# Layer 0's first modulation weights in quarters with two projection blocks joined, and attention weights turned two rows behind their scores

## The chip, the cores and the metric

The kernel runs on one core of a Trainium2 chip. Its time is device microseconds of one execution. The engines are PE (matrix multiplies and transposes, results in PSUM), DVE (elementwise and reductions), ACT (activations and casts), POOL (gathers and small work), and SP, whose queue issues nearly all DMAs. A line number such as L246 is a line of the kernel before; lines of the changed kernel are named as such.

## The reference, cut to what matters

One step of a two-layer trunk over 128 context tokens and 512 latent tokens (640 rows, five token tiles of 128), model width 1024. Each layer is a mixer and an expert channel mixer (PEER), each behind a normalisation that is scaled and shifted by a modulation vector:

```python
sh1, sc1, g1, sh2, sc2, g2 = modulation(c, ada_w[l], ada_b[l])      # silu(c) @ w + b, 6 x 1024 columns
h = rmsnorm(xs, norm_mix_g[l]) * (1.0 + sc1) + sh1
# layer 0: aq, ak, av, bq, bk, bv, br, bg = split(h @ w_in)
#   A: windowed attention, 8 query heads on 2 key heads, softmax with a sink
#   B: gated linear attention in chunks of 64, scanned forwards and backwards
# layer 1: differential attention, 8 heads, two maps
xs = xs + g1 * o
xs = xs + g2 * peer(rmsnorm(xs, norm_ffn_g[l]) * (1.0 + sc2) + sh2, ...)
```

Context and latent rows have a modulation vector each, so a modulation is a product with two columns.

## The kernel before

Products of full precision are made of three passes: a matrix is split into a high part (ACT casts, `w_hi`, `hh`) and a low part (DVE subtracts, `w_lo`, `hl`), and `hi*hi`, `lo*hi`, `hi*lo` are added in PSUM. Normalised tokens are kept transposed, `hh` and `hl`, in eight chunks of 128 features.

`mix0` is layer 0's mixer. Its front works in this order. `Stats` squares the tokens chunk by chunk and adds (ACT and DVE), `end` sums over features on PE (`stin`, L178), and `rs_rows` spreads the reciprocal root over the partitions (`dg` on DVE, `rb` on PE, L203). `ada_half` (L110 to L131) makes the first third of layer 0's modulation in two halves: 8 tiles of 512 KB each, every one two DMAs (L118) into a pool of three buffers, two matmuls a tile (`adap`, L121), a copy of the row (L124), transposes (`adah`, L127), and the addition of the bias (`mods`, L131). `fold_gain` and `norm_mod` (L210 to L213) then give the four chunks of that half, on DVE and ACT. After the first half, four of the five token tiles of projection block 0 (256 query columns) take their first four chunks (`first`, L246); the rest follows when the second half is done.

The projection is in blocks of 256 columns. `proj_t` (tokens on partitions: blocks 0 and 1 queries, 2 keys and values, 3 and 4 values of B; `et`, L246) makes 24 matmuls a token tile; `rope.unit` normalises and rotates queries and keys on DVE, and PE turns them (`utp`, L448). `proj_f` (features on partitions, `ef`, L435) gives B's queries, keys and output gate. The order is blocks 0, 1, 2, the gate `bg` and `z`, then `proj_f(0)`, `proj_f(1)`, blocks 3 and 4, `proj_f(2)`, `proj_f(3)`. A weight block of 1 MB is loaded (L218), cast and split (`wload`, L219, L220).

The next stage has 20 units of attention A (a query block and a pair of heads) in rows r = 0 to 24, in PE's order as written. In a row: `a_scores` (`S`, L552), `a_soft` (maxima on DVE, exponentials on ACT L581, division on DVE L589), the transposes of the weights of unit r-1 (`a_turn`, `PT`, L598, copied by ACT to `pt`), the product of unit r-2 (`a_out`, `oA`, L611). Between them stand B's parts: `scan_setup` (cumulative gates `bT`, L632, and `kps`) in rows 3k and 3k+1, `scan` in row 3k+2 (products `kvb`, L683, then nine dependent DVE steps into `ss`, L688), `b_out` from row 12 (`aT` L704, `oB`, `ost` L738, `orb` L748). `fill` steps give PE the other modulation thirds: each step is a 512 KB tile (`adaw`, L91; `adap`, L94) out of three buffers; the last step loads and splits the first block of the output projection, whose first product is `ewops` (L335).

Layer 1's attention begins with `CS` (L1016), the maximum `cm` on DVE and the exponential `CP` on ACT. Ahead of its first cycle `proj.load(0)` loads output weights and splits them at once (`w_hi` L219 on ACT, `w_lo` L220 on DVE).

## Times and profile before

| | us |
|---|---|
| three runs | 4010.91, 4010.84, 4004.29 |
| median of the runs | 4010.84 |
| profiled execution, its own time | 4004.18 |
| its span | 4002.4 |
| PE busy | 3874.9 (97%) |
| DVE, ACT, POOL busy | 2951.8, 1553.3, 730.9 |
| chain that ended last | PE 75%, DVE 15%, ACT 4%, DMA 3% |

The runs lie on two levels 0.17% apart, and the profiled execution is on the lower one. A busy share says how long an engine had an instruction in it; what a stage costs is read from the idle time of the engine on which it ends, and from the event that ended that idle time. In timelines a row may stand for several records; a matmul of 32-bit operands leaves two records. The granted clock is the share of TensorE's full 2.4 GHz; 0.50 is 1.2 GHz.

### The profile page before, as it was taken

How to read it: one execution, taken by the hardware profiler on the slowest of the kernel's cores; microseconds unless marked ns; L12 is line 12 of the kernel's file. 1: busy time of each engine (PE TensorE's matmuls, PEld its weight loads, DVE VectorE, ACT ScalarE, POOL GpSimd, SP SyncE). 2: the span in 40 equal slices, each digit the busy share in tenths (PEclk: the TensorE clock that was granted, in tenths of full speed). 3: DMA queues.
4: the chain of work that ended last, by engine and by line, in shares of the span. 5: the costliest groups of instructions: out<-in, count | busy, mean ns of one | idle time of the engine just before them, and what ended most of it. 6: DMA issues, size and time to landing. Idle time of an engine off the chain costs nothing.

```text
span 4002.4 us, 55592 instructions
## 1 busy us (share of the span) xinstructions
PE 3874.9 (97%) x20858; PEld 3191.0 (80%) x20858; DVE 2951.8 (74%) x6091; ACT 1553.3 (39%) x2310; POOL 730.9 (18%) x687
## 2 busy tenths in 40 slices
PE   7989999999999999999999899999999999999998
PEld 5958887888788888888877678788878888888887
DVE  5255389996778778777775663999967777787775
ACT  3344235666332323323343553356562323223231
POOL 0000000000334333333200110000003333343432
PEclk9999999999999999999999999999999999999999
DMA  5144134557888888888553012455568888888884
GB/s 181 55 168 143 54 123 170 202 198 255 287 281 296 284 289 304 272 298 285 199 184 107 17 38 70 131 181 202 196 252 294 280 296 297 278 301 276 294 296 169
DMA packets 363922, 850.70 MB, mean 213 GB/s; under 512 B 27858, under 2 KB 172164, under 8 KB 356868
## 3 DMA queue, kind: packets, MB, share of 16 engines
q1 hardware_dynamic: 289012, 576.04, 41.3%
q0 software_dynamic: 74640, 271.10, 19.6%
q8 instruction: 164, 2.69, 0.3%
q14 instruction: 106, 0.87, 0.1%
HBM read 738.12 MB, written 108.92 MB: 212 GB/s over the span
## 4 chain that ended last, share of the span: by engine, by line
PE 75%; DVE 15%; ACT 4%; DMA 3%; issue 2%; POOL 1%; SPq 0%; DVEq 0%; ACTq 0%; POOLq 0%
PE O L1568 11%; PE O L1564 11%; PE O L1565 11%; PE S L1177 8%; PE S L1178 7%; PE S L1180 7%; PE ow L929 4%; PE pqs L1236 2%; PE et L246 2%; DVE ul L220 2%; DMA gr<-Sd 1%; PE ef L435 1%; PE ewops L335 1%; PE owops L335 1%; PE adap L94 1%
## 5 line engine op out<-in xcount | busy, mean ns | idle before, releaser
L1177 PE MATMUL S<-h2h,uh 128*128 128x512 f32 x2048 | 811.0, 396 | 13.2 <-ACT uh L219 5.7
L1564 PE MATMUL O<-Wh,vh 128*128 128x512 f32 x2048 | 798.5, 390 | 6.2 <-ACT Wh L1527 4.5
L1178 PE MATMUL S<-h2l,uh 128*128 128x512 f32 x2048 | 798.8, 390 | 0.0
L1565 PE MATMUL O<-Wh,vl 128*128 128x512 f32 x2048 | 797.9, 390 | 0.0
L1568 PE MATMUL O<-Wl,vh 128*128 128x512 f32 x2048 | 782.2, 390 | 0.0
L1180 PE MATMUL S<-h2h,ul 128*128 128x512 f32 x2048 | 589.2, 389 | 0.0
L219 ACT CAST vh<-v_raw 128x1024 fp32r<-128x1024 f32 x256 | 269.7, 1053 | 804.0 <-PE O L1568 779.8
L1471 POOL DMA_INDIRECT gv<-in_pv_dram,eidx x256 | 362.5, 1416 | 799.2 <-DVE acc L1487 773.7
L1177 PEld LDWEIGHTS S<-h2h,uh 128*128 128x128 f32 x2048 | 385.3, 188 | 98.9 <-ACT uh L219 12.3
L1564 PEld LDWEIGHTS O<-Wh,vh 128*128 128x128 f32 x2048 | 385.0, 188 | 88.1 <-ACT Wh L1527 6.5
L1568 PEld LDWEIGHTS O<-Wl,vh 128*128 128x128 f32 x2048 | 385.3, 188 | 80.4
L1565 PEld LDWEIGHTS O<-Wh,vl 128*128 128x128 f32 x2048 | 385.2, 188 | 79.5
L1180 PEld LDWEIGHTS S<-h2h,ul 128*128 128x128 f32 x2048 | 384.3, 188 | 79.8
L1178 PEld LDWEIGHTS S<-h2l,uh 128*128 128x128 f32 x2048 | 385.5, 188 | 76.6
L220 DVE TENSOR_TENSOR ul<-u_raw,uh 128x1024 fp32r<-128x1024 f32 x256 | 312.2, 1220 | 181.1 <-ACT uh L219 138.9
L1471 POOL DMA_INDIRECT gu<-in_pu_dram,eidx x256 | 320.6, 1252 | 514.6 <-DVE dots L1478 366.5
L219 ACT CAST uh<-u_raw 128x1024 fp32r<-128x1024 f32 x256 | 269.2, 1052 | 336.8 <-PE S L1178 299.6
L220 DVE TENSOR_TENSOR vl<-v_raw,vh 128x1024 fp32r<-128x1024 f32 x256 | 312.4, 1220 | 117.3 <-ACT vh L219 116.2
L1487 DVE SCALAR_TENSOR_TENSOR acc<-gv,dots,acc 128x1024 f32<-128x1024 f32 x256 | 327.7, 1280 | 44.5 <-DMA gv<-in_pv_dram,eidx 43.7
L1478 DVE CUSTOM_DVE_ANT_0 gu<-gu,h2p 128x1024 f32<-128x1024 f32 x256 | 311.2, 1219 | 43.9 <-DMA gu<-in_pu_dram,eidx 43.5
L1402 ACT ACTIVATE stg<-G 128x512 f32<-128x512 f32 x256 | 261.1, 1162 | 0.6 <-PE G L1400 0.6
L1465 POOL MEMSET acc<- 128x1024 f32 x2 | 1.9, 958 | 1335.2 <-DVE oj L1385 757.3
(404 smaller groups left out, 5617.4 us busy)
## 6 DMA issues: line engine op xcount, KB each, us to landing
u_raw<-in_uT_dram SPq DMA_DIRECT2D x256, 512.0 KB, 5.0
v_raw<-in_vR_dram SPq DMA_DIRECT2D x256, 512.0 KB, 6.7
gt<-Gd SPq DMA_DIRECT2D x64, 1024.0 KB, 7.4
Gd<-stg SPq DMA_DIRECT2D x30, 2048.0 KB, 8.5
adaw<-in_adaw_dram SPq DMA_DIRECT2D x80, 512.0 KB, 4.1
Sd<-ge SPq DMA_DIRECT2D x144, 256.0 KB, 3.3
gr<-Sd SPq DMA_DIRECT2D x134, 256.0 KB, 8.7
owr<-in_ow_dram SPq DMA_DIRECT2D x12, 1024.0 KB, 6.5
```

Source lines behind the costliest of these rows:

```text
L219: nc.scalar.copy(hi, raw)
L220: nc.vector.tensor_tensor(lo, raw, hi.bitcast(F32), op=OP.subtract)
L1177: nc.tensor.matmul(ps, hi[:, c], h2h[:, c], start=(c == 0), stop=False)
L1178: nc.tensor.matmul(ps, hi[:, c], h2l[:, c], start=False, stop=False)
L1180: nc.tensor.matmul(ps, lo[:, c - 5], h2h[:, c - 5], start=False, stop=(c == NC + 5 - 1))
L1402: nc.scalar.activation(stg[0][:, :, t0:t0 + 4].rearrange("p i t -> p t i"), ps, AF.Copy, scale=1.0 / GSC)
L1471: nc.gpsimd.indirect_dma_start(out=r[:], out_offset=None, in_=I[table], in_offset=bass.IndirectOffsetOnAxis(ap=eidx2[:, k:k + 1], axis=0))
L1478: nc.vector.tensor_tensor_reduce(r, r, h2p, 1.0, 0.0, OP.mult, OP.add, dots[:, k:k + 1])
L1487: nc.vector.scalar_tensor_tensor(acc, r, dots[:, k:k + 1], acc, op0=OP.mult, op1=OP.add)
L1564: nc.tensor.matmul(ps, hi[:, order[y]], Wh, start=(y == 0), stop=False)
L1565: nc.tensor.matmul(ps, lo[:, order[y]], Wh, start=False, stop=False)
L1568: nc.tensor.matmul(ps, hi[:, x], Ws[n // NC * CH + x][1], start=False, stop=(y == CH + lag - 1))
```

## The change

Three places change; the experts, layer 1's projections and all outputs are computed as before.

1. **The front.** The modulation third comes in four quarters of 8 tiles of 256 KB. All 32 tiles have a place of their own in tiles that are still unused then (`rooms`: the later homes of qA, br, bv, lg, qB, kB and the `adaw` buffers), but for the fourth quarter, which takes the places of the first again. Two chunks are normalised behind each quarter. Blocks 0 and 3 are loaded side by side as 512 columns (`eload`, four chunks at a time), and `emm` multiplies chunk by chunk for all five token tiles, in PE's order as written. The sums over features stand behind the first quarter's matmuls. Blocks 1, 4, 2 follow. There are five PSUM buffers of a bank in place of four.
2. **Attention A with B.** The scan stands at the start of its row, the weights of unit r-2 are turned (before: r-1), the product is that of unit r-3, and each row has 2 fill steps, 5 from row 22 on. Buffers: 5 `Pm`, 4 `pt`, 4 `adaw`, 1 `ktt`; several short-lived tiles share one place.
3. **Layer 1's attention.** The first output weights are loaded ahead (`fetch`) and split at the end of cycle 5.

```diff
-    def ada_half(h, ap, ps, out):
+    def ada_quarter(n, ps, out, tiles, arow):
-        for c in range(NC):
-            if c == 4:
-                yield
-            w = ap.tile([P, 2, 512], F32, name=f"adax{h}_{c}", tag="adaw", bufs=3)
-            for k in range(2):
-                nc.sync.dma_start(w[:, :, k * 256:k * 256 + 256], I["adaw"][0, 0, c, k, :, h::2])
+        for c, w in enumerate(tiles):
+            nc.sync.dma_start(w, I["adaw"][0, 0, c, n % 2, :, n // 2::2])
+        yield
+        r = slice(n % 2 * 64, n % 2 * 64 + 64)
+        for c, w in enumerate(tiles):
             for x in range(2):
-                p0 = h * 64 + x * 32
-                nc.tensor.matmul(ps[p0:p0 + 32], sc[:, c], w[:, x], start=(c == 0), stop=(c == NC - 1))
+                p0 = r.start + x * 32
+                nc.tensor.matmul(ps[p0:p0 + 32, :256], sc[:, c], w[:, x], start=(c == 0), stop=(c == NC - 1))
...
+                def eload(h):
+                    lo, hi = [wp.tile([P, 4, 512], F32R, name=f"e{x}{h}", tag=f"w{x}", bufs=2) for x in "lh"]
+                    raw = wp.tile([P, 4, 512], F32, name=f"er{h}", tag="wr", bufs=1)
+                    for k, b in enumerate((0, 3)):
+                        nc.sync.dma_start(raw[:, :, k * 256:k * 256 + 256], I["ewt"][b][:, h * 4:h * 4 + 4])
+                    store_split(hi, lo, raw)
+                    return hi, lo
...
+                def quarter_end(n):
+                    next(qs[n])
+                    fold_gain(0, 1, gmix, amix[0], n * 2, n * 2 + 2)
+                    norm_mod(0, amix[0], 0, hh, hl, tp, rb, n * 2, n * 2 + 2)
...
+                    def emm(c, tts):
+                        hi, lo = ew[c // 4]
+                        for tt in tts:
+                            a = (slice(None), c, slice(tt * P, (tt + 1) * P))
+                            for k, (x, y) in enumerate(((hh, hi), (hl, hi), (hh, lo))):
+                                nc.tensor.matmul(first[tt], x[a], y[:, c % 4], start=(c == 0 and k == 0),
+                                                 stop=(c == NC - 1 and k == 2))
+                    for n in range(3):
+                        emm(n * 2, range(NT))
+                        if n == 0:
+                            next(qs[3])
+                        next(qs[n + 1])
+                        emm(n * 2 + 1, (0, 1))
+                        quarter_end(n + 1)
+                        emm(n * 2 + 1, (2, 3, 4))
+                    for tt in range(NT):
+                        emm(6, (tt,))
+                        emm(7, (tt,))
...
-                for b in range(3):
+                for tt, ps in enumerate(first):
+                    tsl = slice(tt * P, (tt + 1) * P)
+                    nc.scalar.copy(bv[:, tt, :256], ps[:, 256:])
+                    qk(ps, 0, 0, tt, f"00_{tt}", qA[:, 0:2, tsl])
+                for b in (1, 4, 2):
                     proj_t(b)
...
                 proj_f(1)
-                proj_t(3)
-                proj_t(4)
...
                 for r in range(25):
-                    if r < len(us):
-                        a_scores(us[r])
+                    if r in sq:
+                        scan(*sq[r])
                     for g in row.get(r, []):
                         next(g)
                     if r < len(us):
+                        a_scores(us[r])
                         a_masks(us[r])
                         a_soft(us[r])
-                    if 0 <= r - 1 < len(us):
-                        a_turn(us[r - 1], 0)
+                    if 0 <= r - 2 < len(us):
+                        a_turn(us[r - 2], 0)
                     for g in full.get(r, []):
                         next(g, None)
-                    for _ in range(3 if r % 3 == 0 else 2):
+                    if 0 <= r - 2 < len(us):
+                        a_turn(us[r - 2], 1)
+                    for _ in range(2 if r < 22 else 5):
                         next(fill, None)
-                    if 0 <= r - 1 < len(us):
-                        a_turn(us[r - 1], 1)
-                    if 0 <= r - 2 < len(us):
-                        a_out(us[r - 2])
-                    if r in sq:
-                        scan(*sq[r])
+                    if 0 <= r - 3 < len(us):
+                        a_out(us[r - 3])
...
-                proj.load(0)
+                fins.append(proj.fetch(0))
...
-                        if p_ in (len(units), len(units) + 1):
+                        if p_ in (5, len(units), len(units) + 1):
                             fins.pop(0)()
```

The DMAs of the front as they stand in SP's queue, first before, then now (`adax`, and now `qA` to `adax`, are the modulation tiles; `w_raw` and `er` are projection weights):

```order
L118 DMA adax_0_163<-in_adaw_dram 128x2x256 x2
L118 DMA adax_1_168<-in_adaw_dram 128x2x256 x2
L118 DMA adax_2_173<-in_adaw_dram 128x2x256 x2
L218 DMA w_raw<-in_ewt_dram 128x2048
L118 DMA adax_3_178<-in_adaw_dram 128x2x256 x2
L118 DMA adax_4_212<-in_adaw_dram 128x2x256 x2
```

```order
L114 DMA qA_108<-in_adaw_dram 128x2x256 x4
L114 DMA br_109<-in_adaw_dram 128x2x256 x4
L420 DMA er_183<-in_ewt_dram 128x4x256 x2
L114 DMA bv_110<-in_adaw_dram 128x2x256 x4
L114 DMA lg_111<-in_adaw_dram 128x2x256 x4
L420 DMA er_198<-in_ewt_dram 128x4x256 x2
L114 DMA qB_112<-in_adaw_dram 128x2x256 x2
L114 DMA kB_113<-in_adaw_dram 128x2x256 x2
```

Two quarters, 16 pieces, are now ahead of the second projection load (`er_198`), and the third and fourth quarters stand behind it; that load goes into the one `er` buffer and so waits until the first is split.

PE in rows 2 and 3 of the attention stage, before and now (`S` scores, `PT` turned weights, `bT` gates of the next scan, `kvb` products of the scan, `oA` output, `adap` a fill tile):

```order
L598 MATMUL PT_1_0_1977<-ident,P_1_0_1918 128x128
L94 MATMUL adap_1_1890<-adaw_1_2_1_1981,sc 32x256 x4
L94 MATMUL adap_1_1890<-adaw_1_3_0_1987,sc 32x256 x4
L598 MATMUL PT_1_1_1993<-ident,P_1_1_1920 128x128
L611 MATMUL oA_1997<-pt_0_0_1930,av 64x128
L611 MATMUL oA_1997<-pt_0_1_1956,av 64x128
L683 MATMUL kvb_2001<-bv,ktt_1932 64x128 x16
L683 MATMUL kvx_2002<-bv,ktt_1932 64x128 x2
L552 MATMUL S_3_0_2031<-kA,qA 128x128
L552 MATMUL S_3_1_2032<-kA,qA 128x128
L598 MATMUL PT_2_0_2050<-ident,P_2_0_1967 128x128
L632 MATMUL bT_2054<-tri,lg 128x128 x5
```

```order
L740 MATMUL kvb_1859<-bv,ktt_1836 64x128 x16
L740 MATMUL kvx_1860<-bv,ktt_1836 64x128 x2
L609 MATMUL S_2_0_1889<-kA,qA 128x128
L609 MATMUL S_2_1_1890<-kA,qA 128x128
L655 MATMUL PT_0_0_1908<-ident,P_0_0_1776 128x128
L655 MATMUL PT_0_1_1912<-ident,P_0_1_1778 128x128
L94 MATMUL adap_1_1804<-adaw_1_2_0_1916,sc 32x256 x4
L94 MATMUL adap_1_1804<-adaw_1_2_1_1922,sc 32x256 x4
L609 MATMUL S_3_0_1928<-kA,qA 128x128
L609 MATMUL S_3_1_1929<-kA,qA 128x128
L655 MATMUL PT_1_0_1947<-ident,P_1_0_1826 128x128
L689 MATMUL bT_1951<-tri,lg 128x128 x5
```

Between `kvb` and the next `bT` stood the scores of one row and one transpose; now the scores of two rows, three transposes and two fill tiles stand there, and `PT` takes weights whose scores lie two rows back.

PE at the end of the stage, before and now (`ost` and `orb` belong to the last tile of B's output):

```order
L611 MATMUL oA_3290<-pt_3_0_3400,av 64x128
L611 MATMUL oA_3290<-pt_3_1_3430,av 64x128
L738 MATMUL ost_3499<-ones,obt 128x1 x4
L102 MATMUL adap_0_3014<-ident,adar_0_3511 128x8 x4
L748 MATMUL orb_3518<-obt,ones 128x128 x4
L335 MATMUL ewops_3548<-oh_1815,ewo_h 128x320
```

```order
L668 MATMUL oA_3232<-pt_3_0_3313,av 64x128
L668 MATMUL oA_3232<-pt_3_1_3337,av 64x128
L805 MATMUL orb_3407<-obt,ones 128x128 x4
L94 MATMUL adap_0_3127<-adaw_0_6_1_3415,sc 32x256 x4
L94 MATMUL adap_0_3127<-adaw_0_7_0_3421,sc 32x256 x4
L94 MATMUL adap_0_3127<-adaw_0_7_1_3427,sc 32x256 x4
L102 MATMUL adap_0_3127<-ident,adar_0_3433 128x8 x4
L344 MATMUL ewops_3462<-oh_1729,ewo_h 128x320
```

Three fill tiles and the modulation's transposes (L102) now stand between the last `orb` and `ewops`; before, all fill tiles were ahead of this `oA`.

## Rows read from the trace of the kernel before

**Rows 1.** The page, part 2: PE busy, 40 slices of 100 us.

```profile
PE   7989999999999999999999899999999999999998
```

**Rows 2.** Waits of PE, 0 to 118 us: total us, times, longest.

```profile
PE adap L121 <- DMA adax<-in_adaw_dram: 7.1, 7, 2.7
```

**Rows 3.** Waits of the SP queue from 0 to 130 us.

```profile
SPq L118 <- PE adap L121: 16.1, 12, 6.4
```

**Rows 4.** Groups of PE, 205 to 372 us: busy, mean ns, idle before.

```profile
L94 PE MATMUL adap<-adaw,sc 128*32 128x256 f32 x384 | 26.6, 396 | 2.9 <-DMA adaw<-in_adaw_dram 2.4 <-DVE mods L104 0.6
L598 PE MATMUL PT<-ident,P 128*128 128x128 f32 x120 | 22.3, 298 | 4.7 <-DVE P L589 4.6
...
L552 PE MATMUL S<-kA,qA 64*128 64x256 f32 (+2 forms) x80 | 18.1, 464 | 4.0 <-ACT P L581 3.3 <-ACT br L479 0.7
...
L748 PE MATMUL orb<-obt,ones 128*128 128x128 f32 x40 | 7.2, 339 | 4.0 <-DVE obt L744 4.0
L632 PE MATMUL bT<-tri,lg 128*128 128x128 f32 x40 | 6.6, 321 | 8.7 <-DVE ss L688 3.4 <-DVE mx L577 2.9 <-DVE mx L584 2.5
...
L704 PE MATMUL aT<-qd,kd 64*128 64x128 f32 x80 | 5.5, 277 | 2.7 <-DVE ss L688 2.7
```

**Rows 5.** Windows: us; busy PE, PEld, DVE, ACT, POOL; PE clock, DMA, GB/s.

```profile
8.00:20.00 12.00, 6.18 (x26) 5.20 (x28) 4.56 (x10) 5.24 (x7) 0.00 (x0) 1.00 0.91 310
38.00:42.00 4.00, 4.00 (x15) 1.76 (x11) 4.00 (x10) 2.45 (x6) 0.00 (x0) 0.60 0.79 245
55.00:60.00 5.00, 3.22 (x12) 1.78 (x8) 1.77 (x7) 0.58 (x1) 0.00 (x0) 0.50 0.64 228
...
2226.00:2240.00 14.00, 11.75 (x40) 7.45 (x41) 10.72 (x25) 6.10 (x15) 4.06 (x15) 0.52 0.11 39
```

**Rows 6.** DMA issues: count, KB each, median us to landing.

```profile
adaw<-in_adaw_dram SPq DMA_DIRECT2D x80, 512.0 KB, 4.1
...
adax<-in_adaw_dram SPq DMA_DIRECT2D x32, 256.0 KB, 3.9
```

**Rows 7.** Timeline, 8 to 56 us: start, us, operation, [idle before, released by].

```profile
9.29 4.41 SPq L118 DMA_DIRECT2D adax<-in_adaw_dram  x6
...
12.92 2.29 PE L178 MATMUL stin<-ones,sqin_acc 128*128 128x1 f32 x10 [12.92 <-DVE sqin_acc L172]
...
17.91 1.07 DVE L201 TENSOR_SCALAR dg<-ident,rsn 128x128 f32<-128x128 f32 x5
...
33.05 1.05 PE L121 MATMUL adap<-adax,sc 128*32 128x512 f32 x4 [0.72 <-DMA adax<-in_adaw_dram]
...
36.55 1.01 DVE L210 SCALAR_TENSOR_TENSOR nxr<-xT,amix,rb 128x128 f32<-128x128 f32 x2
...
40.24 1.00 DVE L210 SCALAR_TENSOR_TENSOR nxr<-xT,amix,rb 128x128 f32<-128x128 f32 x2
...
53.57 2.29 DVE L220 TENSOR_TENSOR w_lo<-w_raw,w_hi 128x2048 fp32r<-128x2048 f32 x1 [9.56 <-ACT w_hi L219]
```

**Rows 8.** Timeline of PE: last tile of block 0, and 512-column matmuls elsewhere.

```profile
70.05 0.39 PE L246 MATMUL et<-w_hi,hh 128*128 128x256 f32 x1 [1.21 <-DVE ua L283]
...
2216.25 0.39 PE L929 MATMUL ow<-owh,hh 128*128 128x512 f32 x1
2216.48 0.39 PE L929 MATMUL ow<-owh,hl 128*128 128x512 f32 x1
```

**Rows 9.** The chain of waits, 60 to 210 us: start, us, what.

```profile
148.76 28.80 PE et L246 x240
```

**Rows 10.** Timeline of PE, end of that stage.

```profile
370.02 0.61 PE L335 MATMUL ewops<-oh,ewo_h 128*128 128x320 f32 x1
```

**Rows 11.** Timeline, 2224 to 2227 us, start of layer 1's attention.

```profile
2224.56 1.04 ACT L219 CAST w_hi<-w_raw 128x1024 fp32r<-128x1024 f32 x1 [2.52 <-DMA w_raw<-in_owo_dram]
...
2225.64 1.23 DVE L220 TENSOR_TENSOR w_lo<-w_raw,w_hi 128x1024 fp32r<-128x1024 f32 x1 [0.98 <-ACT w_hi L219]
...
2226.44 2.50 PE L1016 MATMUL CS<-kC,qC 64*128 64x320 f32 x8 [3.22 <-ACT CP L1030]
```

More of the change, by code (lines that the diff above doesn't have):

```diff
@@ L96, in ada @@
                 yield
-        row = ap.tile([P, 512], F32, name=f"adar{l}_{q}", tag="adar", bufs=1)
+        row = (arow or (lambda nm: ap.tile([P, 512], F32, name=nm, tag="adar", bufs=1)))(f"adar{l}_{q}")
         nc.scalar.copy(row, ps)
@@ L391, in mix0 @@
                 tp = s2.enter_context(tc.tile_pool(reuse_waits="tile", name="t0", bufs=2))
-                with ExitStack() as s3:
-                    sp = s3.enter_context(tc.tile_pool(reuse_waits="tile", name="st0", bufs=2))
-                    st = Stats.pooled("in", sp, PP.tile([P, 512], F32, "stin", "b1"), None)
-                    for c in range(NC):
-                        st.add(c)
-                    aps = ada_ps(0, 0)
-                    halves_ = [ada_half(h, ap, aps, pp.tile([P, 2, P], F32, name=f"adah{h}", tag="tr", bufs=1)[:, 0])
-                               for h in range(2)]
-                    next(halves_[0])
-                    st.end()
@@ new lines, in mix0 @@
+                with tc.manual_schedule(engines={mybir.EngineType.PE}):
+                    with ExitStack() as s3:
+                        sp = s3.enter_context(tc.tile_pool(reuse_waits="tile", name="st0", bufs=2))
+                        st = Stats(PP.tile([P, 512], F32, "stin", "b1"),
+                                   act.tile([P, T], F32, name="sqin_acc", tag="bg"),
+                                   lambda c: sp.tile([P, T], F32, name=f"sqin_{c}", tag="sq", bufs=2), None)
+                        for c in range(NC):
+                            st.add(c)
+                        next(qs[0])
+                        ew = [eload(0)]
+                        next(qs[1])
+                        ew.append(eload(1))
+                        next(qs[2])
+                        next(qs[0])
+                        st.end()
+                    rs_rows("0", tp, rb)
+                    quarter_end(0)
+                    first = [PP.tile([P, 512], F32, f"et0_{tt}", "b1") for tt in range(NT)]
+                    def emm(c, tts):
[16 more added lines that the diff above has]
+                        emm(7, (tt,))
@@ L513, in ada_rest @@
                 for l, q in ((0, 1), (0, 2), (1, 0)):
-                    yield from ada(l, q, ap, ada_ps(l, q), 3)
-                hi, lo = [ap.tile([P, NC, P], F32R, name=f"ewo_{x}", tag="adaw", bufs=3) for x in "hl"]
-                w_first.extend(split(ap, hi, lo, I["ewo"][0], P, "ewo", 3, tag="adaw"))
+                    yield from ada(l, q, ap, ada_ps(l, q), 4, arow)
+                hi, lo = [ap.tile([P, NC, P], F32R, name=f"ewo_{x}", tag="adaw", bufs=4) for x in "hl"]
+                w_first.extend(split(ap, hi, lo, I["ewo"][0], P, "ewo", 4, tag="adaw"))
                 yield
```

88 lines of the change are left out of this document (47 added, 41 removed).

## The prediction, made before the changed kernel ran

> **What bounds the kernel now.** I read the page's slices first: PE is the engine on which nearly every slice ends, and only the first four of forty are below nine tenths for it, so a change in layer 0's mixer is worth what it takes out of PE's idle time there [rows 1]. Second the waits of PE in the front: 7.1 us in seven waits for modulation tiles [rows 2]. SP's own waits tell why they are late: it stood 16.1 us, twelve times, until a matmul had freed one of three tile buffers [rows 3]. Third the groups of PE in the attention stage, 205 to 372 us. Their idle times are 2.9, 4.7, 4.0, 4.0, 8.7 and 2.7, together 27.0 us: the next scan's gates `bT` and the first `aT` wait for DVE, which is still in the scan or the maxima, `PT` waits for the divided weights, the last `orb` for the last product of B [rows 4]. Fourth the granted clock: after stretches with waits TensorE runs at 1.2 GHz for a while, 0.60 on average from 38 to 42 us, 0.50 from 55 to 60 [rows 5]. So the bound is not PE's work but the order in which it gets its operands.
>
> **The front, step by step.** The eight pieces of the first quarter are issued 4.41/6 = 0.735 us apart from 9.29 on, the last at 14.4, and land 3.9 us later, at about 18.5 [rows 6, 7]. By the 310 GB/s that flowed from 8 to 20 us their 2.1 MB would take 6.8 us, so issue and landing decide, not the rate [rows 5].
>
> The Trainium skill's page "DMA: Bandwidth & Descriptors", section "Bandwidth", asks for batches of 1 MiB and gives 138 GB/s for a transfer of 64 KB; it would speak against 32 pieces of 256 KB. By an estimate from that figure the four quarters would take 61 us, the fourth would land at 70, and the joined blocks would end near 83 in place of 80 (below). The trace disagrees for pieces of this size: 310 GB/s with several in flight [rows 5].
>
> A tile of 512 columns costs PE 1.05 us, so one of 256 half of it, 0.53, and a quarter 4.2 [rows 7]. The first ends at 19. The sums over features, before begun at 12.92, now stand behind it. From their begin to the end of `dg` it took 18.98 - 12.92 = 6.1 us, so `dg` now ends at 25.1, and with the spreading, the bias and the gains DVE could normalise from 27 [rows 7]. There the low half of the first projection weights stands ahead of it, 2.29 us for a tile of 2048 elements a partition, the size of the new one [rows 7]. The first joined matmul starts at about 32. From there PE has 120 matmuls of 512 columns, 0.23 apart (2216.25 to 2216.48), 27.6 us [rows 8], and three quarters, 12.6: together 40.2, to 72 if nothing waits.
>
> It will wait. From the end of a half's last tile (33.05 + 1.05) to the first normalising instruction there are 2.45 us, and two chunks take 40.24 - 36.55 = 3.7 on DVE, half of that until the first is ready: 4.3 us, against 15 matmuls (3.4 us) that stand beside them [rows 7]. About 1 us a quarter stays open, 3 in all; the fourth leaves 1 more, since both of its chunks must be ready for the last matmuls. Block 1's weights are cast and split meanwhile on ACT and DVE, ahead of the fifth chunk: 4 more (2.29 on DVE and a like time on ACT). I get 32 + 40 + 8 = 80. One fall of the clock as at 55 us, five microseconds at half rate, is likely among these waits; it adds 2.5, so 82.5 [rows 5].
>
> The end to compare it with: before, the last token tile of block 0 began at 70.05 and took 24 matmuls and two transposes, to 73.1 [rows 8]. Blocks 3 and 4 took 28.80 us later, 14.4 for one, 0.12 a matmul [rows 9]. As block 3 is now inside the joined blocks, break-even is 73.1 + 14.4 = 87.5, and the front gains 5.0. Doubling the columns is worth only 120 x (2 x 0.12 - 0.23), about 1 us of it. Bounds: 79 (one wait fewer, no fall of the clock), and 99 if DVE's chain and a cold clock add up; so -8.5 to +11.5.
>
> SP has all 32 pieces behind each other, and the second projection load waits in the queue until the first is split; the third and fourth quarters stand behind it. If the split is at 29.4, 1 MB and 2.1 MB at 310 GB/s land by 40, and PE asks for the third quarter at about 48: hidden by 8 us. The evacuation of five joined tiles (DVE) lies beside block 1's matmuls, since `first` holds five buffers; if it didn't, one wait like the 1.21 at 70.05 would come [rows 8].
>
> **Attention A with B.** Work for PE is unchanged, so I balance its idle time. A whole row now lies between scan and `bT`, and between scores and `PT`: 8.7 + 2.7 + 4.7 go [rows 4]. What is late next: the scores of the next row wait for the exponentials of this one, since `S` has two buffers and fewer instructions stand between. Such waits were 3.3 us in three, 1.1 each [rows 4]; one in each of the four cycles until row 12 is 4.4. In rows 2, 5, 8 and 11 nothing stands between the two halves of `PT`, so the second waits for ACT's copy; no row has this wait, it lies between 0 and PT's mean wait, 4.7/4 = 1.2, and I take 0.8, 3.2 in all. The first `S` and the modulations stay, 1.3.
>
> The stage's end has a new load: 11 fill tiles in the last three rows. With four buffers, 4.1 us to land and 26.6/48 = 0.55 us on PE, a tile comes every 1.16 us: 12.8 us, of which PE works about 8 [rows 4, 6]. Then the first output weights are loaded into the same buffers, cast and split, of which some 4 us are open before `ewops`, which began at 370.02 [rows 10]. That makes 8.5 in place of the 4.0 of `orb` and 2.4 of the `adaw` waits. Sum 4.4 + 3.2 + 1.3 + 8.5 = 17.4, against 27.0: -9.6. Bounds: no new wait and the end as before, 5.3 of idle, -21.7; eight rows that wait the longest seen, 1.9 each, +1.
>
> **Layer 1's attention.** The cast of output weights waited 2.52 us for its DMA and took 1.04 on ACT, ahead of the first exponential; `CS` waited 3.22 for it [rows 11]. Between 1.04 and 3.22 go; I take 1.8. Its later place, in cycle 5, costs 0 to 1.2 (DVE's 1.23), I take 0.6 [rows 11]. From 2226 to 2240 the clock was 0.52 with 11.75 us of PE work [rows 5]; a shorter wait may save up to 5.6, I count 1. Together -2.2.
>
> **Sum.** -5.0 - 9.6 - 2.2 = -16.8. Against the profiled execution, 4004.2, that is 3987; the median, 4010.8, lies on the upper of two levels of the runs and would give 3994. I take the middle, 3991.
>
> **Rivals.** First, the front gains nothing: DVE's chain of splits and normalising is longer than I made it, and the joined blocks end at 87.5. For it, DVE has four splits of weights and eight chunks there; against it, 8 us of waits are already counted. Then -11.8, 3996. Second, attention's waits only change their owner: the longest waits are as good as any softmax with two `S` buffers can have, and the end of the stage costs more. For it, `S` already waited for `P`; against it, the largest waits were DVE's order, not ACT's pace. Then -7.2, 4000. Third, the clock: PE works in bursts of 3 to 4 us between waits, as it did with single tiles before 38 us, when the clock fell. If the clock stays at 1.2 GHz from 32 us on, the 40.2 us become 80.4, the joined blocks end at 112, and the front loses 25: +13, 4021. It decides from 99.3 on, when 19 of the 40 us are cold. Against it: from 38 to 42 us PE was busy throughout, and a mean of 0.60 says that the full clock came back within them [rows 5].
>
> The Trainium skill's "TensorE: Matmul & The Clock Gate", section "HAM oscillation — how this bites in real kernels", states this rule for loops that wait for each load, and advises to run through all of the summed dimension at once, which the quarters do not. By it this third rival would be the likeliest; the rows at 38 and 55 us agree in kind, but each fall ended.
>
> Fourth, more than I count: the falls of the clock in attention and in layer 1 go with the waits. Then about -28, 3979.
>
> **Chances.** Forecast 0.45, first rival 0.18, second 0.17, third 0.10, fourth 0.10. A measurement of this kernel tells about 0.2%, 8 us, from no change. The forecast's own range is 3980 to 4001. The forecast, the first and the fourth are nearly all faster, of the second four tenths: 0.72. Slower is most of the third, 0.09; the rest, 0.19, no change. The range, 3974 to 4008, leaves out the third rival and a tenth at the ends.
>
> **What would show it.** In the trace after: the last of the joined matmuls near 80 to 83 us (over 88: the first rival), the clock in 32 to 80 (0.50 through most: the third). In attention: `bT` and `aT` without waits for `ss` and `mx`; if `S` waits more than 10 us for ACT, the second holds. The end: `ewops` about 15 us earlier than 370; waits of `adap` for DMA in the last 15 us. `CS` in layer 1 without the wait of 3.22. If the front's three rivals are all wrong and the sum still fails, some stage that I count as unchanged has moved.

## The result and the profile after

Four runs of the changed kernel took 3977.29 to 3983.84 us, median 3979.84, beside 4009.43 before: a ratio of 0.9933 (95% interval 0.9921 to 0.9945). By the ratio that is some 27 us less where 17 were forecast; the medians lie 29.6 apart. The profiled execution's span fell from 4002.4 to 3975.4, and PE's slices look as before [rows 1], so the difference has to be found stage by stage. The kernel before ran 62 more times beside the experiments; they took 4000.7 to 4016.2 us with no gap between the two levels of its first runs, which were chance. The span and the row of PE's slices on the page after:

```profile
span 3975.4 us, 55435 instructions
...
PE   7989999999999999999999899999999999999998
```

For every kernel of this study I read three marks from the view of one tile: the first matmul of `bT` (the gates, begin of the attention stage), of `ewops` (the first output product, its end), and of `CS` (layer 1's attention). From the begin to the end of the stage the windows give PE's busy time and the granted clock; the idle time is the length less the busy time. All 14 kernels have about 1560 PE records of the program's own there (1559 to 1564), so a longer busy time is, in the main, a slower clock. The added constant transposes, where there are any, come on top.

| kernel | gates at | stage | PE busy | PE idle | clock | ratio to before (95%) |
|---|---|---|---|---|---|---|
| before | 206.8 | 163.2 | 136.8 | 26.4 | 0.93 | 1 |
| after | 200.7 | 142.3 | 127.6 | 14.7 | 1.00 | 0.9933 (0.9921 to 0.9945) |
| new front, old attention | 200.5 | 170.1 | 145.7 | 24.4 | 0.89 | 1.0009 (0.9999 to 1.0018) |
| old front, new attention | 207.6 | 142.9 | 129.1 | 13.8 | 0.99 | 0.9950 (0.9936 to 0.9963) |
| after, output weights back | 203.2 | 142.2 | 127.6 | 14.6 | 1.00 | 0.9945 (0.9932 to 0.9959) |
| after, scan last | 203.1 | 158.5 | 135.0 | 23.5 | 0.94 | 0.9964 (0.9951 to 0.9977) |
| after, lag one | 202.0 | 149.4 | 135.5 | 13.9 | 0.93 | 0.9935 (0.9922 to 0.9947) |
| after, fills of before | 203.0 | 137.9 | 128.2 | 9.7 | 0.98 | 0.9914 (0.9899 to 0.9928) |
| after, not joined | 203.8 | 143.9 | 131.8 | 12.1 | 0.96 | 0.9929 (0.9916 to 0.9941) |
| not joined, fills of before | 205.3 | 137.9 | 128.2 | 9.7 | 0.98 | 0.9934 (0.9921 to 0.9948) |
| before, scan first | 207.9 | 157.2 | 136.5 | 20.7 | 0.95 | 0.9983 (0.9974 to 0.9992) |
| before, with PE work in waits | 208.7 | 161.5 | 143.1 | 18.4 | 0.96 | 0.9989 (0.9980 to 0.9998) |
| new front, old attention, with PE work | 201.4 | 164.7 | 148.2 | 16.5 | 0.95 | 0.9982 (0.9974 to 0.9991) |
| after, with PE work | 205.6 | 148.1 | 138.9 | 9.2 | 0.98 | 0.9945 (0.9931 to 0.9958) |

Between the two profiles the gates come 6.1 us earlier and the stage is 20.9 shorter; from `ewops` to `CS` it is 1851.3 and 1853.7, from there to the end 1781.1 and 1778.7, together the same. The whole difference of the two profiles, 27.0 us, thus lies ahead of the end of the attention stage. Over all kernels the last two stretches vary from 1847.4 to 1853.7 and from 1778.3 to 1784.7 without an edit in most of them. A single profile's total is therefore good to a few microseconds only.

**The front after.** The waits of PE up to 110 us, which answer to [rows 2]:

```profile
PE adap L120 <- DMA qA<-in_adaw_dram: 13.6, 2, 13.3
PE et L457 <- DVE hl L222: 4.1, 4, 1.9
PE et L457 <- ACT hh L221: 3.4, 3, 1.7
...
PE adap L120 <- DMA br<-in_adaw_dram: 0.5, 1, 0.5
```

Of the 13.6, 13.3 is the wait at the start, in place of the 12.92 for the sums; the waits between tiles, 7.1 us before, are 0.8 (0.3 of the first line and the 0.5 of the last). What is left are 7.5 us for the normalised chunks. The timeline of PE and DVE (start, us, operation):

```profile
20.88 1.28 PE L187 MATMUL stin<-ones,sqin_acc 128*128 128x1 f32 x10
...
28.88 0.35 DVE L219 SCALAR_TENSOR_TENSOR nxr<-xT,amix,trt 128x128 f32<-128x128 f32 x1
...
29.14 2.28 DVE L309 TENSOR_TENSOR el<-er,eh 128x2048 fp32r<-128x2048 f32 x1
...
29.72 0.80 PE L457 MATMUL et<-eh,hh 128*128 128x512 f32 x1 [1.54 <-ACT hh L221]
...
31.75 0.80 PE L457 MATMUL et<-eh,hl 128*128 128x512 f32 x1 [1.23 <-DVE hl L222]
...
60.50 0.50 PE L457 MATMUL et<-eh,hh 128*128 128x512 f32 x1 [1.71 <-ACT hh L221]
...
62.87 0.51 PE L457 MATMUL et<-eh,hl 128*128 128x512 f32 x1 [1.87 <-DVE hl L222]
...
83.35 0.39 PE L457 MATMUL et<-el,hh 128*128 128x512 f32 x1
...
83.58 0.28 PE L255 MATMUL et<-w_hi,hh 128*128 128x256 f32 x1
```

The sums follow the first quarter at 20.88, the low half of the first weights stands on DVE at 29.14 between two pieces of normalising, PE starts the joined matmuls at 29.72 and gets its first low operand at 31.75, and the last joined matmul starts at 83.35. Ahead of 60.50 and 62.87 PE waits 1.71 and 1.87 us; DVE splits block 1 in between (at 59.86, for 2.29 us). The clock in two windows of this front (columns as in [rows 5]):

```profile
24.00:28.00 4.00, 3.26 (x14) 3.04 (x14) 1.26 (x6) 1.92 (x2) 0.00 (x0) 0.50 1.09 345
64.00:68.00 4.00, 4.00 (x16) 2.36 (x16) 0.55 (x3) 0.00 (x0) 0.00 (x0) 0.57 0.96 394
```

It is at 1.2 GHz from 23 to 37 us and again from 64 to 67, after the waits at 60.

**The attention stage after.** PE's waits from 180 to 372 us, against [rows 4]:

```profile
PE PT L655 <- ACT pt L657: 4.2, 7, 1.0
PE adap L94 <- DMA adaw<-in_adaw_dram: 2.9, 5, 0.8
PE S L609 <- ACT P L638: 2.6, 3, 1.0
PE kps L710 <- ACT kd L704: 2.1, 2, 1.6
PE ewops L344 <- ACT ewo_h L228: 0.9, 1, 0.9
PE aT L761 <- DVE obt L790: 0.8, 2, 0.4
PE adap L102 <- ACT adar L98: 0.7, 1, 0.7
```

The gates and the first output row no longer wait for DVE's scan; the largest wait that is left is for ACT's copy between the two halves of `PT`. The stage as a whole, before and then after, each from its first gates to its first output product:

```profile
206.80:370.00 163.20, 136.83 (x1564) 104.10 (x1561) 98.00 (x280) 79.43 (x193) 0.00 (x0) 0.93 0.48 168
```

```profile
200.70:343.00 142.30, 127.64 (x1561) 96.13 (x1561) 95.59 (x281) 79.44 (x194) 0.00 (x0) 1.00 0.51 186
```

Of 20.9 us, 11.7 are idle time (26.4 to 14.7) and 9.2 are PE's busy time, 136.83 to 127.64 for the same instructions. Before, the clock fell four times in the stage (from about 232, 243, 307 and 366 us on, for 3.5 to 7 us each); after, it doesn't fall between 200 and 343. The profiles of the other five kernels that keep this order (the old front, the output weights put back, the fills of before, and the two with block 0 alone) have 0 to 3 falls and a busy time of 127.6 to 131.8.

A fall costs busy time. Twice before, PE waited for DVE ahead of the ten records of `bT`:

```profile
223.70 1.35 PE L632 MATMUL bT<-tri,lg 128*128 128x128 f32 x10 [2.45 <-DVE mx L584]
243.60 2.47 PE L632 MATMUL bT<-tri,lg 128*128 128x128 f32 x10 [3.38 <-DVE ss L688]
```

At 223.70 the clock stayed at 1.00, at 243.60 it was 0.50. So a wait does not always bring a fall: of the seven waits of 1.8 us and more in this stage before, three had one in or behind them (1.85, 3.38 and 3.99 us) and four had none (2.45, 2.69, 2.88 and 3.00); the fall at 232 stands behind waits of 0.6 and 1.2.

The end of the stage, which answers to [rows 10]:

```profile
338.45 0.64 PE L94 MATMUL adap<-adaw,sc 128*32 128x256 f32 x8 [0.67 <-DMA adaw<-in_adaw_dram]
339.72 0.64 PE L94 MATMUL adap<-adaw,sc 128*32 128x256 f32 x8 [0.63 <-DMA adaw<-in_adaw_dram]
341.06 1.06 PE L102 MATMUL adap<-ident,adar 128*128 128x8 f32 x8 [0.71 <-ACT adar L98]
343.00 0.42 PE L344 MATMUL ewops<-oh,ewo_h 128*128 128x320 f32 x1 [0.88 <-ACT ewo_h L228]
```

**Layer 1's attention after**, against [rows 11] and the last of [rows 5]:

```profile
2200.08 1.72 PE L1072 MATMUL CS<-kC,qC 64*128 64x320 f32 x8 [1.55 <-ACT CP L1086]
```

```profile
2201.00:2215.00 14.00, 11.16 (x67) 7.30 (x65) 12.18 (x32) 8.03 (x18) 5.66 (x23) 1.00 0.00 1
```

The wait is 1.55 in place of 3.22, and the clock stays at 1.00. From the first to the last `CS` product of scores it takes 131.1 to 132.4 us in the seven kernels with the new loading and 132.0 to 133.6 in the seven without: 1.3 us on average.

### The profile page after: what moved, and what is told of

It reads as the page before. It is cut to its first block, busy times and chain, and to the rows that moved or that the text cites. A ratio compares the mean times of both kernels' runs of the same rounds, so it can differ in the third digit from the quotient of the medians.

```text
span 3975.4 us, 55435 instructions
## 1 busy us (share of the span) xinstructions
PE 3864.1 (97%) x20801; PEld 3178.8 (80%) x20801; DVE 2948.8 (74%) x6099; ACT 1552.1 (39%) x2311; POOL 721.8 (18%) x687
## 4 chain that ended last, share of the span: by engine, by line
PE 62%; DVE 15%; issue 11%; DMA 5%; ACT 4%; POOL 3%; SPq 0%; POOLq 0%; DVEq 0%; ACTq 0%
PE O L1624 8%; PE O L1620 8%; PE O L1621 8%; PE S L1233 7%; PE S L1234 7%; PE S L1236 6%; PE ow L985 4%; PE pqs L1292 2%; DMA gu<-in_pu_dram,eidx 2%; DVE ul L229 2%; PE ewops L344 1%; PE ef L492 1%; PE owops L344 1%; POOL gu L1527 1%; POOL gv L1527 1%
```

## The experiments

Theory A: the stages of the two traces may be taken at face value, and the attention gained twice, by waits and by the clock behind them. Its rivals (B: the prediction's sizes and a shift of the runs; C: the attention gained through the front; D: the clock follows something else than waits) are in the expectations.

**The new front alone.** Attention and layer 1 are those of before, in the new buffers.

```diff
-                    if r in sq:
-                        scan(*sq[r])
                     for g in row.get(r, []):
...
-                    if 0 <= r - 2 < len(us):
-                        a_turn(us[r - 2], 0)
+                    if 0 <= r - 1 < len(us):
+                        a_turn(us[r - 1], 0)
...
-                fins.append(proj.fetch(0))
+                proj.load(0)
```

> The new front with the attention order, and layer 1's loading of output weights, of before (the buffers of the attention stage are the new ones). Theory A, that the two traces' stages can be taken at face value (front 3.9 us, the stretch up to the first scores another 2.5 because the gate's products no longer run at 1.2 GHz, attention 20.5): 6 to 7 us below before, ratio 0.998, first scores at 200 us, attention stage 160 to 164 us long with falls of the granted clock to 0.50 in it. Theory B, the sizes of the prediction (front 5, attention 9.6, layer 1 2) with the remaining 10 us coming from a shift of the runs as a whole: also about 5 us below; this run alone tells only the front's share. Theory C, that the attention's gain comes from the front's new order (what is ready earlier): 15 us or more below, stage under 155 us.

Measured 1.0009 (0.9999 to 1.0018): nothing gained, though the gates came at 200.5, 6.3 earlier. All three theories missed the total, and A was wrong to take the old stage's length as given:

```profile
200.50:370.60 170.10, 145.68 (x1560) 110.07 (x1561) 97.49 (x278) 79.65 (x193) 0.00 (x0) 0.89 0.43 152
```

Its idle time is 24.4, less than before; its busy time is 145.7, 8.9 more. The old order kept its waits but they fell on other places, and the clock fell eight times in the stage in place of four. A wait of the same length for the same maxima as the one before at 223.70 now has a fall behind it:

```profile
217.94 2.47 PE L689 MATMUL bT<-tri,lg 128*128 128x128 f32 x10 [2.46 <-DVE mx L641]
```

It is not one execution alone: the mean clock of a whole run was 0.982 to 0.985 in the eleven runs of this kernel, 0.984 to 0.988 in the 21 of the kernel before beside them, and 0.988 to 0.990 in the four of the changed kernel. The front's gain was spent there. Whether the earlier start did it or the new buffers in the old order is not shown, since no run has these buffers with the old front and the old order.

**The new attention alone.** The loop, the buffers and the fills of the change, with the front and layer 1 of before; several short-lived tiles were moved into a shared place to make room.

```diff
-                    Pm = tp.tile([P, 512], F32, name=f"P{nm}_{g}", tag="Pm", bufs=4)
+                    Pm = tp.tile([P, 512], F32, name=f"P{nm}_{g}", tag="Pm", bufs=5)
...
-                    yield from ada(l, q, ap, ada_ps(l, q), 3)
+                    yield from ada(l, q, ap, ada_ps(l, q), 4, arow)
...
+                    if r in sq:
+                        scan(*sq[r])
```

> The front of before (with the tiles that the new attention needs moved into a shared place) and the new attention order with its buffers and fills; layer 1 as before. Theory A: 18 to 22 us below before, ratio 0.995, the stage from the first scores to the first output product 143 to 147 us long in place of 163.6, granted clock 0.98 or more in it. Theory B: about 10 us below, ratio 0.9975, stage near 154. Theory C: less than 8 us below.

0.9950, 20 us, stage 142.9 (143.3 from the first scores), clock 0.99: as theory A had it. The attention's gain does not need the new front; theory C falls. The total's interval overlaps the changed kernel's, so what the front adds is seen in its marks and not in the total.

**The same old order with work in its waits.** If the clock made the stage long, work that fills the waits must shorten it. Transposes of the constant `ident` into a spare tile, which nothing reads (one of three places is shown):

```diff
+                if (d, p) != (0, 0):
+                    dm = pp.tile([P, 512], F32, name=f"dm{nm}", tag="PT")
+                    for x in range(16):
+                        nc.tensor.transpose(dm[:, x % 4 * P:(x % 4 + 1) * P], ident, ident)
                 bp = pp.tile([P, 1024], F32, name=f"bT{nm}", tag="b2")
```

> The kernel before with work added: transposes of a constant that nothing reads, on PE, ahead of the gates of scans 2 to 4 (16 each), of the scores of row 15 (10) and of the last output norm (24), where PE stood idle 1.9 to 4.0 us. Theory A, that the waits cost twice, once as waits and once as a fall of the clock behind them: the falls at 243 to 249, 308 to 314 and 366 to 372 us are gone, the granted clock of the stage rises from 0.93 to 0.97 or more, and the stage gets 3 to 7 us shorter although PE has 2 to 3 us more in each place. Theory D, that the falls belong to something else (the loads, or the stage's transposes): same falls, stage 0 to 8 us longer.

0.9989 (0.9980 to 0.9998) with 82 transposes more in the stage. Two of the places where the clock had fallen before:

```profile
243.00:249.00 6.00, 5.40 (x33) 3.61 (x35) 2.90 (x10) 2.06 (x7) 0.00 (x0) 0.50 0.14 40
308.00:314.00 6.00, 6.00 (x43) 5.88 (x44) 1.89 (x5) 1.38 (x4) 0.00 (x0) 0.50 0.00 0
```

The whole stage now, then three of these places:

```profile
208.70:370.20 161.50, 143.13 (x1645) 108.17 (x1643) 98.07 (x280) 79.32 (x193) 0.00 (x0) 0.96 0.49 168
243.00:249.00 6.00, 5.17 (x57) 4.00 (x55) 4.79 (x16) 2.68 (x8) 0.00 (x0) 1.00 0.13 30
308.00:314.00 6.00, 4.35 (x55) 3.86 (x56) 1.38 (x5) 1.70 (x6) 0.00 (x0) 1.00 0.00 0
366.00:372.00 6.00, 4.68 (x38) 4.47 (x37) 4.59 (x11) 1.42 (x2) 0.00 (x0) 1.00 0.62 227
```

At 243 to 249, 308 to 314 and 366 to 372 us the clock is 1.00 where it was 0.50. Other falls came instead, from 216 and 284 on, for 7 us each. The clock of the stage is 0.96 where 0.97 was expected, and the stage is 1.7 us shorter, not 3 to 7: two falls are left, and PE has the added work besides.

With the new front, and in more places (one is shown):

```diff
+                    if r in (15, 17, 19):
+                        dm = pp.tile([P, 512], F32, name=f"dm{r}", tag="PT")
+                        for x in range(10):
+                            nc.tensor.transpose(dm[:, x % 4 * P:(x % 4 + 1) * P], ident, ident)
                     if r < len(us):
                         a_scores(us[r])
```

> The run with the new front and the old attention order, which came out no faster than before although its first gates came 6.3 us earlier (granted clock of the stage 0.88), with transposes of a constant that nothing reads put on PE ahead of the gates of scans 2 to 4 (16 each), the first output row (12) and the scores of rows 15, 17 and 19 (10 each). Theory A' (falls of the clock behind the waits of the old order ate the front's gain, and how many there are depends on where the waits fall): granted clock 0.95 or more, the stretch from the first gates to the first expert queries, 251.2 us there, falls to 236 to 244, total 6 to 12 us below before. Theory D (the stage is longer for another reason, for example transfers that now collide): 251 or longer, total at or above before.

0.9982 (0.9974 to 0.9991), against 1.0009 without the transposes, and the intervals don't touch:

```profile
201.40:366.10 164.70, 148.19 (x1651) 113.04 (x1651) 97.01 (x278) 79.52 (x193) 0.00 (x0) 0.95 0.45 157
```

The clock is 0.95 in place of 0.89 and the stage 5.4 us shorter although PE executes some 90 instructions more. (The expectation counted to a later mark; to the same mark it is 244.8 in place of 251.2.) Clock and total came out as theory A' had them, the stretch 0.8 us above its range. That is the direct evidence: more work for PE would not shorten a stage that is long because of transfers, so it was the clock that had eaten the front's gain.

**Which part of the new order.** One thing undone at a time in the changed kernel, first the scan's place:

```diff
                 for r in range(25):
-                    if r in sq:
-                        scan(*sq[r])
...
                         a_out(us[r - 3])
+                    if r in sq:
+                        scan(*sq[r])
```

> The changed kernel with one thing undone: the scan stands at its row's end again, the weights are still turned two rows behind. Theory A (the scan's place removed the waits of the gates and of the first output rows, 11.4 us before, and with them the falls of the clock behind them): these waits are back, the stage from the first gates to the first expert queries, 222.1 us in the changed kernel and 243.1 before, gets 10 to 18 us longer, total 0.25 to 0.45% above the changed kernel. Theory E (the lag of the turned weights did it, and the scan's place is neutral): stage within 3 us of the changed kernel.

0.9964, 12 us above the changed kernel, as theory A had it. The waits that came back:

```profile
PE bT L689 <- DVE ss L745: 6.2, 2, 3.2
PE aT L761 <- DVE ss L745: 3.4, 1, 3.4
...
PE bT L689 <- DVE mx L641: 2.5, 1, 2.5
```

12.1 us of waits, of which idle time keeps 8.8 net; busy time is 7.4 longer, and the clock fell five times.

Then the lag:

```diff
-                    if 0 <= r - 2 < len(us):
-                        a_turn(us[r - 2], 0)
+                    if 0 <= r - 1 < len(us):
+                        a_turn(us[r - 1], 0)
...
-                        a_out(us[r - 3])
+                        a_out(us[r - 2])
```

> The changed kernel with the other thing undone: the weights are turned one row behind the scores again and multiplied two rows behind, the scan stays at the row's start. Theory A: the waits of the turned weights for the division (4.7 us before) come back and with them one or two falls, 4 to 10 us longer than the changed kernel, 0.1 to 0.25%. Theory E: 12 us or more longer. If neither alone brings much back, the two overlap: either order gives enough work between the steps.

0.9935: no difference from the changed kernel in the total, so nothing that can be measured is owed to the second row of lag. The waits for the division did come back, but as many others went, idle time is 13.9 against 14.7:

```profile
PE PT L655 <- DVE P L646: 7.0, 5, 2.9
```

Its profiled stage has a clock of 0.93 and is 7.1 us longer, as theory A expected, yet its six runs reach from 3974.7 to 3987.1, below the changed kernel's lowest (3977.3). Whether the lag steadies the clock is not settled.

Then the kernel before with the scan first and nothing else:

```diff
                 for r in range(25):
+                    if r in sq:
+                        scan(*sq[r])
...
-                    if r in sq:
-                        scan(*sq[r])
```

> The kernel before with one edit: the scan stands at its row's start, ahead of the scores; front, lag of one, fill steps, buffers and layer 1 are those of before. Theory A2, formed after the run with the scan put back (12 us slower than the changed kernel) and the run with the lag put back (no difference): the scan's place alone carries the attention's gain, because the gates of the next scan and the first output row no longer meet a scan that is still running; waits of 11.4 us go, the stretch from the first gates to the first expert queries falls from 243.1 to 224 to 233 us, total 10 to 18 us below before, ratio 0.9955 to 0.9975. Rival: it needs the lag or the fills as well, ratio above 0.998.

0.9983 (0.9974 to 0.9992), 7 us; the expectation of 10 to 18 was too high, and the rival is right in part. The waits of the scan are gone, but others took their place:

```profile
PE S L552 <- ACT P L581: 6.9, 7, 1.9
PE PT L598 <- DVE P L589: 6.7, 4, 3.0
PE orb L748 <- DVE obt L744: 4.0, 1, 4.0
```

So the full gain needs the scan's place, and the scan's place alone does not give it: with the scan first and a lag of one row, the stage is 157.2 in the kernel before and 149.4 in the changed one. These two differ in more than the lists above say: besides the front, the fills and the buffers, the changed kernel has the scores behind the gates in a row, and both halves of `PT` ahead of the fill steps. `S` waits 6.9 us for the exponentials in the one and 0.4 in the other. None of these had a run of its own, so which of them carries the rest is open.

**The fills.** In the changed kernel, with one line:

```diff
-                    for _ in range(2 if r < 22 else 5):
+                    for _ in range(3 if r % 3 == 0 else 2):
```

> The changed kernel with the fill steps of before, 3, 2, 2 a row throughout in place of 2 and then 5 from row 22 on. The prediction put 8.5 us of idle time on the new end of the stage, against 6.4 before. If that is right, the end (from the last orb to the first output product) gets 3 to 5 us shorter here and the total stays the same or falls by up to 4 us; if the fills fill waits elsewhere, the early rows change as much the other way. Within 0.1% of the changed kernel either way.

0.9914, the lowest ratio of all, though its interval overlaps the changed kernel's, and the stage is 4.4 us shorter: 137.9, idle 9.7. Its end:

```profile
337.43 1.06 PE L102 MATMUL adap<-ident,adar 128*128 128x8 f32 x8 [0.83 <-ACT adar L98]
338.41 0.88 PE L668 MATMUL oA<-pt,av 128*64 128x128 f32 x12
339.22 2.07 PE L805 MATMUL orb<-obt,ones 128*128 128x128 f32 x8
340.95 0.61 PE L344 MATMUL ewops<-oh,ewo_h 128*128 128x320 f32 x1
```

The one wait there is 0.83; no fill tile waits for its transfer and `ewops` waits for nothing, where the changed kernel has the rows above with 0.67, 0.63, 0.71 and 0.88.

**Joined blocks.** In the changed kernel, block 0 alone is multiplied as it is normalised:

```diff
-                    for k, b in enumerate((0, 3)):
+                    for k, b in enumerate((0,)):
...
-                                nc.tensor.matmul(first[tt], x[a], y[:, c % 4],
+                                nc.tensor.matmul(first[tt][:, :256], x[a], y[:, c % 4],
...
-                for b in (1, 4, 2):
+                for b in (1, 3, 4, 2):
```

> The changed kernel with the quarters, but with block 0 alone (256 columns) multiplied as the chunks are normalised, and block 3 as a block of its own behind block 1; nothing else changes. Theory A: block 3's work lay in waits of the front, so the joined end comes only 3 to 6 us earlier than 83.6 us and 14.4 us are added: first gates 8 to 11 us later than 200.7, total 0.2 to 0.28% above the changed kernel, and the quarters alone would then have cost against before. Rival: the front is bound by PE's work, its end comes 13.8 us earlier and only the width's 1 us is lost.

0.9929: no loss that can be measured. The gates come at 203.8, and the seven kernels with joined blocks (those without added work in the front) have them at 200.5 to 203.2, on average 202.0. The last matmul of this part starts at 70.42 (71.96 in the next run), and at 83.2 to 85.8, on average 84.6, in the seven: 13.4 earlier, where the rival says 13.8 and theory A 3 to 6. The expected 8 to 11 us are wrong; the rival, PE's work as the bound, is borne out.

This edit and the one of the fills together:

> Two single edits of the changed kernel together: block 0 alone in place of the joined blocks 0 and 3, and the fill steps of before (3, 2, 2 a row). Alone, the first measured 0.9929 of before (the changed kernel 0.9933) and the second 0.9914. If the fills' 4.4 us in the stage are real and joining is worth nothing, 0.991 with an interval that reaches to 0.990 to 0.9925, the stretch from the first gates to the first expert queries 217 to 219 us, first gates at 201 to 204 us. If the fills' gain was a lucky set of executions, 0.993 and a stretch of 222.

0.9934 with a stage of 137.9: the fills' gain in the stage is there again, but the total is no lower than without it (0.9929). So a shorter stage is shown twice (142.3 to 137.9, and 143.9 to 137.9); a lower total is not shown, since the intervals overlap each time.

**More work in the changed kernel's waits:**

```diff
+                    for x in range(10):
+                        nc.tensor.transpose(first[0][:, x % 4 * P:(x % 4 + 1) * P], ident, ident)
                     rs_rows("0", tp, rb)
...
+                        if r >= 22:
+                            dm = pp.tile([P, 512], F32, name=f"dm{r}_{_}", tag="PT")
+                            for x in range(4):
+                                nc.tensor.transpose(dm[:, x * P:(x + 1) * P], ident, ident)
                         next(fill, None)
```

> The changed kernel with transposes of a constant that nothing reads on PE: 10 ahead of the spreading of the root, 8 ahead of the first joined matmul, 4 ahead of every fill step from row 22 on, where PE waits. Theory A (the clock falls behind waits and comes back with work): the granted clock of 24 to 36 us, 0.50 in the changed kernel, is back earlier and the joined blocks end 1 to 3 us before 83.6; the fall at 344 us behind the stage's end goes, 1 to 2 us more. Total 0 to 4 us below the changed kernel. If the transposes only cost: 1 to 3 us above.

0.9945: not faster than the changed kernel, nor slower beyond the intervals. In the front:

```profile
20.00:24.00 4.00, 3.80 (x19) 1.96 (x19) 0.00 (x0) 0.00 (x0) 0.00 (x0) 0.61 1.07 351
24.00:28.00 4.00, 4.00 (x20) 4.00 (x21) 0.52 (x3) 2.50 (x4) 0.00 (x0) 0.50 1.10 354
28.00:32.00 4.00, 4.00 (x23) 3.86 (x22) 0.82 (x5) 1.20 (x1) 0.00 (x0) 0.61 0.33 104
36.00:40.00 4.00, 3.78 (x9) 2.11 (x8) 2.57 (x6) 1.64 (x3) 0.00 (x0) 0.50 0.89 246
```

PE had an instruction nearly throughout from 20 to 32 us, and the clock was 0.50 to 0.61 there and 0.50 again at 36; the last joined matmul starts at 88.26, 3.6 later than the others' average, not 1 to 3 earlier. The fall behind the end of the stage did go (1.00 from 343 us on, over the stage's end at 353.7), but the stage is 5.8 us longer, with a busy time of 138.9 in place of 127.6. Here the transposes only cost.

**Output weights.** The third edit undone in the changed kernel:

```diff
-                fins.append(proj.fetch(0))
+                proj.load(0)
...
-                        if p_ in (5, len(units), len(units) + 1):
+                        if p_ in (len(units), len(units) + 1):
```

> The changed kernel with layer 1's output weights loaded and split ahead of the first cycle again. Theory A, by the two traces layer 1's attention took 145 us before and 143.3 now: 1 to 2 us slower than the changed kernel, a wait of about 3 us of the first scores for the exponential and a granted clock near 0.5 behind it. Theory B, the prediction's 2.2: the same. Rival: nothing, because the split only moves, 0 within 1 us.

0.9945 against 0.9933: the intervals overlap, so the total shows nothing. In its trace the wait is 3.41 and the clock behind it 0.52, as before; by the stretch of `CS` above, the edit is worth about 1.3 us on average.

## Why the prediction was right, and where its sizes were off

- **Direction and range.** Faster, and 3979.8 lies in 3974 to 4008. The likeliest time, 3991, was 11 high, and the forecast's own range, 3980 to 4001, was just missed; it is the wider one that holds. What happened is the fourth rival (3979), which had a chance of 0.10. Of the three terms, -5.0, -9.6 and -2.2, the two profiles show -6.1 and -20.9, and for the third nothing that a total can tell.
- **The front's sum.** The joined blocks ended at 83.6 where 82.5 was forecast, with the first low operand at 31.75 (32), the sums' `dg` ready at 25.5 (25.1), and two waits at block 1's split of 3.6 us (4). The sums took half the time that was taken from before (1.28 for a row of ten, not 2.29), and the first quarter came 2 us later; these cancelled. Against the prediction's 87.5 the end at 83.6 is worth 3.9 of the 6.1 us; the rest came behind it, in a stretch that was counted as unchanged, where the clock was down for 7 us before (from 116 on) and for 3.5 now (from 142 on). The 310 GB/s that the prediction takes for pieces of 256 KB are of a window into which SP also issued 1 MB of weights; but with pieces of 256 and 512 KB in SP's queue the changed kernel moved 345 to 356 GB/s from 20 to 28 us, so the reading holds. Over the kernels the gates come 5.8 us earlier (206.8 to 208.7, on average 207.8, in the four with the front of before, 202.0 in the seven with the new one); the forecast was 5.0.
- **Joining.** The prediction gave it about 1 us, for the columns. Unjoined the gates come 2.5 us later (203.8 and 205.3), which is within what kernels with the same front differ by, and no total shows it; by the same marks the quarters alone are worth 3.2 of the front's 5.8. That block 3 fills waits, on which my later expectation rested, is refuted by the end at 70.42.
- **The attention's idle time.** 9.6 forecast, 11.7 measured, by the terms named in other sizes, which partly cancel: waits for ACT's copy 4.2 (3.2), for the exponentials 2.6 (4.4), at the end 4.5 (8.5). A wait not foreseen, `kps` for `kd`, took 2.1. That the new end costs is right: undoing it gives the stage 4.4 back.
- **The step that failed is the clock in that stage.** The prediction said that PE's work is unchanged and balanced only idle time. The same instructions took 9.2 us less. Its rows have the clock of the front and of layer 1's begin [rows 5], and it counted something for each, but no row has the clock of the stage whose waits it removed, and the term was put at nothing; only the fourth rival names it. So the range held by its width, and not because the sum was complete. The second half of the evidence, the front's gain lost in a kernel that keeps the old order, nobody would have got from idle time alone.
- **The third rival**, a cold front, came true for 14 us at its start and 3.5 behind 64; it did not last. The rule of the Trainium skill's "TensorE: Matmul & The Clock Gate", section "HAM oscillation — how this bites in real kernels", agrees in kind with the attention stage of before, but there three of seven waits of 1.8 us and more had slow work behind them, not each. In the front its advice was not followed, and the chunk-by-chunk order still kept the full clock from 37 to 64 us.
- **Layer 1.** 2.2 forecast, about 1.3 measured by its own marks.

## What to carry to other kernels

Where PE waits a few microseconds, price the wait twice: its own length, and the work behind it that may run at 1.2 GHz. Not every wait brings a fall, so read it from the clock of that stage, and read busy time for an equal number of instructions beside idle time. Judge an upstream edit together with the stage that follows: here an earlier start came to nothing while the next stage kept its waits. Place a chain of dependent DVE steps so that a whole row of other work stands before its reader. Filler work saved for the end of a stage made that stage longer here.

## What the runs showed of the hardware

- The same 1560 PE records of one stage took from 127.6 to 145.7 us of busy time, at a granted clock of 1.00 to 0.89; only their order differs. Ten records of `bT` took 1.35 us at 1.00 and 2.47 at 0.50.
- Waits of 2.45 and 2.46 us ahead of the same instructions, in two kernels, were followed by a clock of 1.00 and of 0.50.
- In the first 20 us the granted clock reads 1.00 before PE has done anything; ten records of `stin` took 2.29 us there at 12.92 [rows 7] and 1.28 at 20.88 in the changed kernel. So in these traces a reading of 1.00 ahead of the first change does not tell how fast PE ran.
- Kernels with the same front have their first gates up to 2.7 us apart (200.5 to 203.2), so differences of that size can't be given to an edit from one profile each.
